# A hybrid SSD and neighbourhood-attention block: the scan in 16 steps with 2.5 pieces of the q, k, v projection each

## The chip, the cores and the metric

The kernel runs on one core of one Trainium2 chip. The metric is the device time in microseconds of one execution of the whole program, the median over several runs. The engines of the core are named as in the profile: PE (TensorE, matrix products into the PSUM banks), DVE (VectorE), ACT (ScalarE), POOL (GpSimd) and SP (SyncE, here the queue from which most DMA transfers are issued; ACT has a queue of its own). Each engine works through its own queue in order, and waits on semaphores for what others make.

## The reference, cut to what matters

One encoder layer over T = 1024 tokens of width 1024, all in float32:

```python
h = rmsnorm(x, norm_mix_w)
z, xbc, dt_raw, q, k, v = split(h @ w_in)           # 1024 | 1536 | 32 | 1024 | 1024 | 1024 columns
xs, B, C = split(silu(conv5(xbc)))                   # xs: 16 heads of 64; B, C: 2 groups of 128 states
dt_f, dt_b = softplus(dt_raw + dt_bias)              # one step size per token, head and direction
y = ssd(xs*dt_f, dt_f*a_f, B, C) + flip(ssd(flip(xs*dt_b), flip(dt_b*a_b), flip(B), flip(C))) + d_skip*xs
y_ssm = grouped_rmsnorm(y * silu(z)) * norm_w        # groups of 512 columns
y_na  = neighbourhood_attention(rmsnorm(q), rmsnorm(k), v, rel_pos_bias)
x = x + concat([y_ssm, y_na]) @ w_out
x = x + relu(rmsnorm(x) @ w1)**2 @ w2
```

`ssd` is a chunked scan. In each of 8 chunks of 128 tokens, with `a_cum` the running sum of the log decays:

```python
decay  = exp(where(lower, a_cum[l] - a_cum[s], -inf))        # per head, 128 x 128
y_diag = (C @ B.T * decay) @ xdt                             # inside the chunk
state  = B.T @ (xdt * exp(a_cum[-1] - a_cum))                # what the chunk adds
h      = exp(a_cum[-1]) * h + state                          # carried to the next chunk
y_off  = (C @ h_in) * exp(a_cum)                             # what comes from the chunks before
```

The backward direction is the same on the reversed sequence, so its states are carried from the last chunk to the first.

## The kernel before, in words

**Stages.** The program has these stages one after the other: transposing and splitting x; twelve x tiles (`xbc`, columns of the projection for xs, B and C, each followed by the convolution; B and C come first, then `decays`, then the eight tiles of xs); the gate z in two groups of 8 tiles of tokens; the scan together with the q, k, v projection; the attention with the output projection; the MLP in seven products per block. Exact float32 products are made of three matmuls on a high and a low part (`mm3`, lines 180 to 182; `split_from_psum`, lines 189 and 190): the high part is an ACT copy, the low part a DVE or POOL difference. Weights come as tiles of 128 x 1024 through SP's queue (line 149, `wraw`), are split by ACT (line 150, `wh`) and DVE (line 151, `wl`), and there are three raw buffers and four pairs of split ones, so that one group of 512 columns (four tiles) fills them.

**A piece** is one tile of 128 tokens of one group of 512 columns of q, k or v: 24 matmuls into a bank `mm` (three banks), and after it for q and k a norm (ACT, DVE, POOL), four transposes into a bank `tp` and a split, for v only a split, and stores from ACT's queue. Three projections with two groups of eight make 48 pieces, traced as one loop behind the scan.

**The scan before** goes over i = 0..7 and the groups g = 0, 1, and makes `backward(7 - i, g)` and then `forward(i, g)`:

- `backward` loads xs, makes C B (`pcb`, line 575, a bank `s`), and for each half of the group's 8 heads loads the running sums of both directions, broadcast to all partitions (`rb`, line 593), subtracts the token's own sum (two POOL operations, line 600), selects by the triangle (DVE, line 606), takes the exponential (ACT, line 611), multiplies by C B (DVE, line 613) and makes four heads' products (`pd`, line 618, the one bank `v`). One matrix per head so serves both directions, one in each triangle. Then it adds what the later chunks carry in (`carried`), sums it all up, and updates the backward state (`decay_state`): a weighing of xs on POOL, a split (lines 528 and 529), the products `pS`, POOL and DVE to update the state (lines 537 and 538), and a split of the state (lines 541 and 542).
- `forward` adds what the earlier chunks carry in, and updates the forward state in the same way.
- The half of y that is made first waits in `y1_dr` in DRAM until the other direction reaches that chunk. Then `gated` multiplies with silu(z), norms and stores.

`carried` splits C for each use (lines 550 and 551), multiplies with the split state (`py`, a bank `s`; there are two) and scales (`yo`, line 555, one buffer).

**What sets the order.** The tile framework puts every instruction into its engine's queue by a simulated timeline: an instruction is issued when its inputs are ready in that timeline, and of those ready, the one traced first. So before the change the q, k, v pieces fill PE wherever the planner expects the scan not to be ready. `tc.issue_after(ins)` adds an edge of order alone: what is traced in the block goes behind `ins` on its engine. Buffers are handed on tile by tile (`reuse_waits="tile"`): a new tile waits for the last use of what lay there. The attention's pools lie partly where the scan's tiles were.

Of the kernel before, what the change touches and what calls it, by code (L numbers as in the profile page):

```python
# [19 lines left out]
P = 128  # L20
T = 1024
D = 1024
# [34 lines left out]
def hymba_block(  # L57
# [66 lines left out]
    y1_dr = dr.tile([NT, P, D], F32, name="y1_dr")  # L124
# [54 lines left out]
    def mm3(pt, ah, al, bh, bl, first, last):  # L179
        nc.tensor.matmul(pt, lhsT=ah, rhs=bh, start=first, stop=False)  # L180
        nc.tensor.matmul(pt, lhsT=ah, rhs=bl, start=False, stop=False)  # L181
        return nc.tensor.matmul(pt, lhsT=al, rhs=bh, start=False, stop=last)  # L182

# [24 lines left out]
    with ExitStack() as ph:  # L208
# [21 lines left out]
        with ExitStack() as p0:  # L230
# [14 lines left out]
            for h in range(2):  # L245
# [31 lines left out]
                dg = rp.tile([P, 4, P], F32, tag="dg", name="dg")  # L277
# [29 lines left out]

        def proj_col(get, m, h, pt):
# [5 lines left out]
        with p1:  # L314
            qp = p1.enter_context(tc.tile_pool(name="qp", bufs=2, side="right", reuse_waits="tile"))
# [166 lines left out]
            for ft in range(8):  # L482
                xbc((ft,))


            szb = sz_dr.rearrange("c p f -> (c p) f").rearrange(
                "(i b j) f -> i b j f", b=8, j=8
            )
            for g in range(2):
                get = load_w_nat(w_in[0], 0, KD, OFF_Z + 512 * g, nc.vector)  # L490
                for t in range(NT):
                    pt = ps_mm("pz")
                    for k in range(KD):
                        s = (slice(None), k, slice(t * P, (t + 1) * P))
                        mm3(pt, hTh[s], hTl[s], *get(k), k == 0, k == KD - 1)
                    zs = qp.tile([P, 512], F32, tag="zs", name="zs")
                    nc.scalar.activation(zs, pt, AF.Silu, scale=rcol[:, t : t + 1])
                    nc.scalar.dma_start(szb[:, t, :, g * 512 : (g + 1) * 512], zs)

        def hb(v):  # L500
            return v.unsqueeze(2).broadcast_to([P, 8, HD])

        def h8(v):
            return v.rearrange("p (e d) -> p e d", d=HD)

        with ExitStack() as p2:
# [14 lines left out]
            st = [[None, None], [None, None]]  # L521

            def decay_state(d, c, g, xw):
                prev = st[d][g]
                pS = ps_s("pS")
                xh = qp.tile([P, 512], F32R, tag="xh", name="xh", bufs=1)
                xl = qp.tile([P, 512], F32R, tag="xl", name="xl", bufs=1)
                nc.scalar.activation(xh, xw, AF.Copy)
                nc.vector.tensor_tensor(xl, xw, xh.bitcast(F32), op=sub)
                mm3(pS, bNh[:, c, g, :], bNl[:, c, g, :], xh, xl, True, True)  # L530
                new = prev and prev[0]
                if prev is None:
                    new = qp.tile([P, 512], F32, tag=f"st{d}{g}", name="st", bufs=1)
                    nc.vector.tensor_copy(new, pS)
                else:
                    dec = ed[:, d, c, 8 * g : 8 * g + 8]
                    nc.gpsimd.tensor_tensor(h8(new), h8(new), hb(dec), op=mul)
# [183 lines left out]

# [680 lines left out]
```

## Time and profile before

| what | value |
|---|---|
| median of 3 runs | 1670.96 us (1668.05 to 1673.75) |
| the profiled execution: its time, its span | 1675.21 us, 1673.4 us |
| mean granted PE clock of the profiled execution | 0.988 |
| x tiles from `decays` on, about 84 to 172 us | 88 us, PE busy throughout |
| the gate z, 172 to 261 us | 89 us, PE busy throughout |
| scan with pieces, 261 to 600 us | 339 us, PE 306.0, DVE 270.0, POOL 264.5, ACT 134.9 us busy |
| pieces alone, 600 to 668 us | 68 us |

The table is read by stage: busy time of an engine in a stretch, against the stretch's length. A matmul of 512 columns is reported with about 390 ns, though in a dense stream one starts every 227 ns, because matmuls overlap; so for PE the distances between starts count, not the durations. Where a wait of PE is reported, it names the instruction that PE waited with and the one that released it.

### The profile page before, as it was taken

Reading aid. Unit: us, or ns where it says so; the run is one execution under the profiler, and the core shown is the slowest. Engines: PE = TensorE matmul, PEld = TensorE weight load, DVE = VectorE, ACT = ScalarE, POOL = GpSimd, SP = SyncE. Lnnn points to the kernel's source line nnn. Section 1 sums busy time; section 2 is a strip of 40 time slices with the busy share of each in tenths; the row PEclk is TensorE's granted clock in tenths of the full one; section 3 lists DMA queues with packets and bytes.
Section 4 is the critical chain, followed back from the end, with each engine's and each line's share of the span. In section 5 each row is a group of like instructions: output and inputs, shape, how many; then the busy total and the mean of one; then the engine's idle time right before and its main releaser. Section 6 shows DMA issues by size and latency. Waiting matters only on the chain. (4 is left out here: it accounts for less than half of the span.)

```text
span 1673.4 us, 20880 instructions
## 1 busy us (share of the span) xinstructions
PE 1594.3 (95%) x7462; PEld 1296.9 (78%) x7462; DVE 1027.3 (61%) x1432; ACT 722.5 (43%) x1195; POOL 721.8 (43%) x520
## 2 busy tenths in 40 slices
PE   7999999899998899999999989999999979999999
PEld 6788888777776677887887777788888868888887
DVE  4777214889796852666675567434243388887863
ACT  5434223434343442566665433554444444433330
POOL 3000004788688762233334232344444465455551
PEclk9999999999999999999999999999999999999999
DMA  8113337776666884987674240343354386644331
GB/s 206 52 38 114 87 99 226 208 193 195 223 216 185 225 266 176 279 212 204 174 208 133 89 164 38 138 164 131 133 166 149 129 295 230 219 145 151 101 101 76
DMA packets 181026, 273.49 MB, mean 163 GB/s; under 512 B 14691, under 2 KB 105915, under 8 KB 180923
## 3 DMA queue, kind: packets, MB, share of 16 engines
q1 hardware_dynamic: 136939, 231.26, 45.3%
q10 hardware_dynamic: 42976, 37.23, 7.3%
q0 software_dynamic: 1008, 3.67, 0.5%
q8 instruction: 59, 0.97, 0.2%
q14 instruction: 44, 0.36, 0.1%
HBM read 188.88 MB, written 86.56 MB: 165 GB/s over the span
## 5 line engine op out<-in xcount | busy, mean ns | idle before, releaser
L748 POOL TENSOR_TENSOR wl<-wraw,wh 128x1024 fp32r<-128x1024 f32 x110 | 298.8, 2728 | 318.4 <-ACT wh L747 305.1
L747 ACT ACTIVATE wh<-wraw 128x1024 fp32r<-128x1024 f32 x110 | 115.5, 1054 | 151.3 <-PE px L733 51.3
L733 PE MATMUL px<-wh,ahl 128*128 128x512 f32 x512 | 160.9, 391 | 4.6 <-ACT ahl L747 3.3
L180 PE MATMUL pq<-wh,hTh 128*128 128x512 f32 x384 | 152.7, 400 | 4.8 <-ACT wh L150 4.8
L181 PE MATMUL pq<-wl,hTh 128*128 128x512 f32 x384 | 152.3, 398 | 5.2 <-DVE wl L151 5.2
L733 PE MATMUL px<-h,wh 128*128 128x512 f32 x496 | 155.8, 394 | 1.4 <-DVE x L1089 1.4
L182 PE MATMUL pq<-wh,hTl 128*128 128x512 f32 x384 | 152.0, 397 | 0.0
L748 DVE TENSOR_TENSOR ahl<-ar,ahl 128x1024 fp32r<-128x1024 f32 x56 | 114.8, 2058 | 23.2 <-ACT ahl L747 22.1
L747 ACT ACTIVATE ahl<-ar 128x1024 fp32r<-128x1024 f32 x56 | 58.2, 1052 | 140.0 <-PE px L733 76.3
L733 PEld LDWEIGHTS px<-wh,ahl 128*128 128x128 f32 x512 | 96.1, 188 | 26.0 <-ACT ahl L747 3.7
L733 PEld LDWEIGHTS px<-h,wh 128*128 128x128 f32 x496 | 92.8, 187 | 24.4 <-ACT h L186 1.6
L151 DVE TENSOR_TENSOR wl<-wraw,wh 128x1024 fp32r<-128x1024 f32 x40 | 54.7, 1373 | 82.5 <-ACT wh L150 81.9
L733 PE MATMUL px<-wl,ahl 128*128 128x512 f32 x256 | 99.9, 390 | 0.0
L733 PE MATMUL px<-h,wl 128*128 128x512 f32 x248 | 97.8, 394 | 0.0
L181 PEld LDWEIGHTS pq<-wl,hTh 128*128 128x128 f32 x384 | 72.9, 190 | 22.2 <-DVE wl L151 8.0
L180 PEld LDWEIGHTS pq<-wh,hTh 128*128 128x128 f32 x384 | 72.8, 190 | 21.5 <-ACT wh L150 7.1
L186 ACT ACTIVATE pth<-ptp 128x384 fp32r<-128x384 f32 (+1 forms) x128 | 56.8, 456 | 67.1 <-PE ptp L947 66.6
L600 POOL TENSOR_TENSOR rb<-rb,c 128x512 f32<-128x512 f32 x64 | 76.1, 1210 | 20.3 <-DMA rb<-cum_dr 17.4
L182 PEld LDWEIGHTS pq<-wh,hTl 128*128 128x128 f32 x384 | 72.9, 190 | 14.7
L150 ACT ACTIVATE wh<-wraw 128x1024 fp32r<-128x1024 f32 x58 | 61.0, 1057 | 53.1 <-PE px L181 24.1
L733 PE MATMUL pz<-h,wh 128*128 128x512 f32 x256 | 81.9, 400 | 0.7 <-DVE h L187 0.7
L733 PE MATMUL pz<-wh,ahl 128*128 128x512 f32 x256 | 80.5, 391 | 0.0
(271 smaller groups left out, 4081.2 us busy)
## 6 DMA issues: line engine op xcount, KB each, us to landing
ar<-act_dr SPq DMA_DIRECT2D x56, 512.0 KB, 3.6
act_dr<-cq SPq DMA_DIRECT2D x49, 512.0 KB, 3.0
wraw<-in_w_in_dram SPq DMA_DIRECT2D x44, 512.0 KB, 4.3
rb<-cum_dr SPq DMA_DIRECT2D x32, 512.0 KB, 6.7
wraw<-in_w_mlp_in_dram SPq DMA_DIRECT2D x32, 512.0 KB, 4.6
wraw<-in_w_mlp_out_dram SPq DMA_DIRECT2D x32, 512.0 KB, 4.2
q_dr<-hl ACTq DMA_DIRECT2D x64, 128.0 KB, 3.0
k_dr<-hl ACTq DMA_DIRECT2D x16, 512.0 KB, 4.4
```

Source lines behind the costliest of these rows:

```text
L150: nc.scalar.activation(hi[:, 0:n], raw[:, 0:n], AF.Copy)
L151: lo_eng.tensor_tensor(lo[:, 0:n], raw[:, 0:n], hi[:, 0:n].bitcast(F32), op=sub)
L180: nc.tensor.matmul(pt, lhsT=ah, rhs=bh, start=first, stop=False)
L181: nc.tensor.matmul(pt, lhsT=ah, rhs=bl, start=False, stop=False)
L182: return nc.tensor.matmul(pt, lhsT=al, rhs=bh, start=False, stop=last)
L186: top = nc.scalar.activation(hi, src, AF.Copy)
L600: nc.gpsimd.tensor_tensor(rb[:, d], rb[:, d], c1[:, d, c, h0 : h0 + 4].unsqueeze(2).broadcast_to([P, 4, P]), op=sub,)
L733: nc.tensor.matmul(pt, lhsT=a, rhs=b, start=f, stop=l, skip_group_check=True)
L747: nc.scalar.activation(hl[0], src, AF.Copy)
L748: eng.tensor_tensor(hl[1], src, hl[0].bitcast(F32), op=sub)
```

## The change

The scan is laid out anew:

- **Exponents.** `segment` makes the differences of the decays for four heads of a chunk (broadcast load, two POOL subtractions, the DVE selection) and stores them to `seg_dr` in DRAM. One of the 32 is made after each of the eight x tiles of xs, one after each of the 16 tiles of z, and the last eight in the first eight steps of the scan. The exponential itself is taken after loading, in the scan.
- **Backward states.** Beside z, `state_in` loads xs, weighs and splits it, and two tiles of z later `state_out` makes the products, updates the running backward state and stores it to `sb_dr`, one for each of the 14 chunks that need one.
- **Steps.** The scan is now one pass over g and, inside it, c, 16 steps in forward order. `prepare` makes what a step needs besides the forward state (loads, exponentials, splits of C, of the stored backward state and of the weighed xs) and is traced a step ahead. `inside` makes C B (now in a bank `tp`), both `py` products and most of the sum; `carry` updates the forward state behind a piece; `finish` makes the heads' products behind the same piece, and the gating. `y1_dr` is gone; every chunk is finished in its step.
- **Pieces.** The q, k, v projection is a generator of 48 pieces. One is traced before the first step, two or three in each step, and the last seven after the scan.
- Buffers: `yo` has two, and the tiles for z move from the pool `qp` to `rp`.

```diff
+            def segment(pool, bufs, g, c, q):
+                h0 = 8 * g + 4 * q
+                rb = pool.tile([P, 2, 4, P], F32, tag="rb", name="rb", bufs=bufs)
+                r0 = c * 16 + h0
+                nc.sync.dma_start(
+                    rb.rearrange("p d h s -> p d (h s)"),
+                    cum_dr[:, r0 : r0 + 4, :]
+                    .rearrange("d h s -> d (h s)")
+                    .partition_broadcast(P),
+                )
+                for d in range(2):
+                    nc.gpsimd.tensor_tensor(
+                        rb[:, d],
+                        rb[:, d],
+                        c1[:, d, c, h0 : h0 + 4].unsqueeze(2).broadcast_to([P, 4, P]),
+                        op=sub,
+                    )
+                nc.vector.copy_predicated(
+                    rb[:, 0],
+                    lmask.unsqueeze(1).broadcast_to([P, 4, P]),
+                    rb[:, 1],
+                )
+                nc.sync.dma_start(seg_dr[g, c, :, q], rb[:, 0].rearrange("p h s -> p (h s)"))
+
+            segs = [(g, c, q) for g in range(2) for c in range(NT) for q in range(2)]
...
             for ft in range(8):
                 xbc((ft,))
+                segment(rp, 2, *segs.pop(0))
...
+            def weighed(pool, bufs, d, c, g, xs):
+                xw = pool.tile([P, 512], F32, tag="xw", name="xw", bufs=bufs)
+                hs = slice(8 * g, 8 * g + 8)
+                nc.gpsimd.tensor_tensor(h8(xw), h8(xs), hb(wd[:, d, c, hs]), op=mul)
+                hl = [pool.tile([P, 512], F32R, tag=f"x{i}", name="xhl", bufs=bufs) for i in "hl"]
+                split_to(hl, xw, nc.vector)
+                return hl
+
+            def state_in(c, g):
+                xs = zp.tile([P, 512], F32, tag="xs", name="xs")
+                nc.sync.dma_start(xs, xs_dr[c, :, g * 512 : (g + 1) * 512])
+                return c, g, weighed(zp, 2, 1, c, g, xs)
+
+            def state_out(c, g, hl):
+                pS = ps_s("pS")
+                mm3(pS, bNh[:, c, g, :], bNl[:, c, g, :], *hl, True, True)
+                new = zp.tile([P, 512], F32, tag="st", name="st")
+                if g not in sb:
+                    nc.vector.tensor_copy(new, pS)
+                else:
+                    nc.gpsimd.tensor_tensor(
+                        h8(new), h8(sb[g]), hb(ed[:, 1, c, 8 * g : 8 * g + 8]), op=mul
+                    )
+                    nc.vector.tensor_tensor(new, new, pS, op=add)
+                sb[g] = new
+                nc.sync.dma_start(sb_dr[g, c - 1], new)
...
                     nc.scalar.dma_start(szb[:, t, :, g * 512 : (g + 1) * 512], zs)
+                    n = 8 * g + t
+                    if n > 1:
+                        with tc.issue_after(mark.ins):
+                            state_out(*ready.pop(0))
+                    if n < 14:
+                        ready.append(state_in(NT - 1 - n % 7, n // 7))
+                    segment(rp, 2, *segs.pop(0))
...
+            def prepare(c, g):
...
+                nc.sync.dma_start(xs, xs_dr[c, :, gs])
+                for q in range(2):
+                    gm = qp.tile([P, 4, P], F32, tag=f"gm{q}", name="gm")
+                    nc.sync.dma_start(gm.rearrange("p h s -> p (h s)"), seg_dr[g, c, :, q])
+                    nc.scalar.activation(gm, gm, AF.Exp)
...
+                split_to(chl, ct, nc.vector)
+                if c < NT - 1:
...
+                    nc.sync.dma_start(raw, sb_dr[g, c])
...
+                    split_to(back, raw, nc.vector)
+                    xhl = weighed(qp, 1, 0, c, g, xs)
...
+            def inside(c, g, xs, gms, chl, sts):
+                pcb = ps_tp("pcb")
...
+                for d in sts:
+                    pys[d] = ps_s("py")
+                    mm3(pys[d], *chl, *sts[d], True, True)
...
+                nc.gpsimd.tensor_tensor(h8(y1), h8(xs), hb(cf), op=mul)
+                for gm in gms:
+                    nc.vector.tensor_tensor(
+                        gm, gm, cb.unsqueeze(1).broadcast_to([P, 4, P]), op=mul
+                    )
+                for d in sts:
+                    yo = qp.tile([P, 512], F32, tag="yo", name="yo")
+                    nc.vector.tensor_tensor(h8(yo), h8(pys[d]), hb(e1[:, d, c, hs]), op=mul)
+                    nc.gpsimd.tensor_tensor(y1, y1, yo, op=add)
+
+            def carry(c, g, xhl, mark):
+                pS = ps_s("pS")
+                with tc.issue_after(mark):
+                    mm3(pS, bNh[:, c, g, :], bNl[:, c, g, :], *xhl, True, True)
...
+                    nc.gpsimd.tensor_tensor(h8(st[g]), h8(st[g]), hb(dec), op=mul)
+                    nc.vector.tensor_tensor(st[g], st[g], pS, op=add)
+                hl = [qp.tile([P, 512], F32R, tag=f"s{i}", name="shl", bufs=1) for i in "hl"]
+                split_to(hl, st[g], nc.vector)
+
+            def finish(c, g, xs, gms, y1, mark):
+                pd = ps_v("pd")
+                with tc.issue_after(mark):
+                    for e in range(8):
+                        nc.tensor.matmul(
+                            pd[:, e * HD : (e + 1) * HD],
+                            lhsT=gms[e // 4][:, e % 4, :],
+                            rhs=xs[:, e * HD : (e + 1) * HD],
+                            start=True,
+                            stop=True,
+                        )
+                nc.vector.tensor_tensor(y1, y1, pd, op=add)
+                gated(y1, c, g)
...
+            steps = [(c, g) for g in range(2) for c in range(NT)]
+            held = prepare(*steps[0])
+            mark = next(units)
+            ahead = {}
+            for n, (c, g) in enumerate(steps):
+                xs, gms, chl, back, xhl = held
+                sts = {}
+                if back:
+                    sts[1] = back
+                if c > 0:
+                    sts[0] = ahead[g]
+                y1 = inside(c, g, xs, gms, chl, sts)
+                if n + 1 < len(steps):
+                    held = prepare(*steps[n + 1])
+                mark = next(units)
+                if xhl:
+                    ahead[g] = carry(c, g, xhl, mark)
+                finish(c, g, xs, gms, y1, mark)
+                mark = next(units)
+                if segs:
+                    segment(qp, 1, *segs.pop(0))
+                if n % 2:
+                    mark = next(units)
+            for mark in units:
+                pass
```

More of the change, by code (lines that the diff above doesn't have):

```diff
@@ L276, in hymba_block @@
                 nc.gpsimd.tensor_tensor(rcol[:, s], rcol[:, s], half[:, s], op=ALU.pow)
[L277 removed]
+                dg = rp.tile([P, 4, P], F32, tag="zs", name="dg", bufs=2)
                 nc.vector.tensor_tensor(
@@ L306, in hymba_block, with hb, h8 @@
         nc.sync.dma_start(dsk, d_skip.partition_broadcast(P)[:, 0, :])
+        def hb(v):
+            return v.unsqueeze(2).broadcast_to([P, 8, HD])
+        def h8(v):
+            return v.rearrange("p (e d) -> p e d", d=HD)
         def proj_col(get, m, h, pt):
@@ L494, in hymba_block @@
                         s = (slice(None), k, slice(t * P, (t + 1) * P))
-                        mm3(pt, hTh[s], hTl[s], *get(k), k == 0, k == KD - 1)
-                    zs = qp.tile([P, 512], F32, tag="zs", name="zs")
+                        mark = mm3(pt, hTh[s], hTl[s], *get(k), k == 0, k == KD - 1)
+                    zs = rp.tile([P, 512], F32, tag="zs", name="zs", bufs=2)
                     nc.scalar.activation(zs, pt, AF.Silu, scale=rcol[:, t : t + 1])
                     nc.scalar.dma_start(szb[:, t, :, g * 512 : (g + 1) * 512], zs)
[L500 to L504, printed above, removed]
+                    n = 8 * g + t
[5 more added lines that the diff above has]
+                    segment(rp, 2, *segs.pop(0))
         with ExitStack() as p2:
@@ L567, in gated @@
                 nc.scalar.dma_start(y_dr[c, :, gs], y1)
-            def backward(c, g):
+            def prepare(c, g):
+                gs = slice(g * 512, (g + 1) * 512)
+                xs = qp.tile([P, 512], F32, tag="xs", name="xs")
+                nc.sync.dma_start(xs, xs_dr[c, :, gs])
+                gms = []
+                for q in range(2):
+                    gm = qp.tile([P, 4, P], F32, tag=f"gm{q}", name="gm")
+                    nc.sync.dma_start(gm.rearrange("p h s -> p (h s)"), seg_dr[g, c, :, q])
+                    nc.scalar.activation(gm, gm, AF.Exp)
+                    gms.append(gm)
+                ct = cT[:, g, c * P : (c + 1) * P]
+                chl = [qp.tile([P, P], F32R, tag=f"c{i}", name="chl") for i in "hl"]
+                split_to(chl, ct, nc.vector)
+                back = None
+                if c < NT - 1:
+                    raw = qp.tile([P, 512], F32, tag="sb", name="sb", bufs=1)
+                    nc.sync.dma_start(raw, sb_dr[g, c])
+                    back = [
+                        qp.tile([P, 512], F32R, tag=f"b{i}", name="shl", bufs=1) for i in "hl"
+                    ]
+                    split_to(back, raw, nc.vector)
+                    xhl = weighed(qp, 1, 0, c, g, xs)
+                else:
+                    xhl = None
+                return xs, gms, chl, back, xhl
+            def inside(c, g, xs, gms, chl, sts):
                 hs = slice(8 * g, 8 * g + 8)
                 cs = slice(c * P, (c + 1) * P)
-                xs = qp.tile([P, 512], F32, tag="xs", name="xs")
-                nc.sync.dma_start(xs, xs_dr[c, :, g * 512 : (g + 1) * 512])
-                pcb = ps_s("pcb")
+                pcb = ps_tp("pcb")
                 nc.tensor.matmul(
```

186 lines of the change are left out of this document (53 added, 133 removed).

## The prediction

> **What bounds the kernel now.** I read the engine totals first, then busy time by stretches, then who waited for whom on TensorE (PE) in the stretch that the change rebuilds, and last the order of single matmuls, for the price of each kind. Totals and stretches:
>
> ```profile
> span 1673.4 us, 20880 instructions
> PE 1594.3 (95%) x7462; PEld 1296.9 (78%) x7462; DVE 1027.3 (61%) x1432; ACT 722.5 (43%) x1195; POOL 721.8 (43%) x520
> ...
> 84.00:172.00 88.00, 88.00 (x421) 73.16 (x420) 62.35 (x75) 37.44 (x43) 0.51 (x8) 1.00 0.27 78
> 172.00:261.00 89.00, 89.00 (x402) 73.90 (x401) 14.44 (x13) 23.24 (x29) 0.26 (x1) 1.00 0.32 88
> 261.00:600.00 339.00, 306.00 (x1452) 245.61 (x1451) 270.01 (x389) 134.88 (x240) 264.50 (x243) 0.97 0.73 212
> 600.00:640.00 40.00, 36.39 (x168) 29.17 (x167) 17.88 (x24) 13.80 (x21) 19.40 (x22) 1.00 1.01 306
> 640.00:668.00 28.00, 28.00 (x129) 23.27 (x129) 5.70 (x8) 6.72 (x9) 2.37 (x2) 1.00 0.36 139
> ```
>
> The columns of a stretch are its bounds and length, then busy us of PE, weight loads, DVE (VectorE), ACT (ScalarE) and POOL (GpSimd), the granted clock, the DMA share and GB/s. The x tiles (84 to 172) and the gate z (172 to 261) leave PE no idle time, and POOL has nothing to do there. From 261 to 600 the scan runs between the q, k, v pieces, and there PE idles for 33 us, DVE is busy for 80% and POOL for 78%. Then the rest of the pieces runs until 668. So PE is the bound, and only the 407 us from 261 to 668 hold time to win. Who held PE there:
>
> ```profile
> PE pd L618 <- DVE rb L613: 7.3, 7, 2.3
> PE pcb L575 <- DVE yo L555: 6.6, 4, 2.5
> PE pq L181 <- DVE wl L151: 5.2, 7, 1.8
> PE pq L180 <- ACT wh L150: 4.8, 4, 2.1
> PE pd L618 <- issue: 3.0, 1, 3.0
> PE py L180 <- DVE yo L555: 2.3, 2, 1.7
> PE ptq L693 <- DVE qn L687: 2.0, 5, 1.0
> PE py L181 <- DVE sl L542: 1.7, 2, 1.2
> PE py L180 <- DVE st L538: 1.0, 1, 1.0
> PE pS L180 <- ACT rb L611: 0.8, 1, 0.8
> PE ptq L693 <- ACT sz L564: 0.8, 1, 0.8
> PE pS L180 <- DVE st L538: 0.8, 1, 0.8
> ```
>
> After the colon stand the total us, the number of waits and the longest. The twelve rows add up to 36.3 us. Now the price of each kind of PE work, from the order in time:
>
> ```profile
> 280.41 1.10 PE L618 MATMUL pd<-xs,rb 128*128 128x64 f32 x8 [0.99 <-DVE rb L613]
> 281.32 0.48 PE L180 MATMUL pS<-xh,bNh 128*128 128x512 f32 x1
> ...
> 282.18 0.39 PE L575 MATMUL pcb<-cT,bT 128*128 128x128 f32 x2
> 282.40 0.60 PE L693 MATMUL ptq<-ident,qn 128*128 128x128 f32 x4
> 282.76 0.48 PE L180 MATMUL pq<-wh,hTh 128*128 128x512 f32 x1
> ...
> 308.71 0.39 PE L182 MATMUL pq<-wh,hTl 128*128 128x512 f32 x1
> ...
> 309.62 0.39 PE L180 MATMUL py<-sh,ch 128*128 128x512 f32 x1
> ...
> 310.30 0.39 PE L180 MATMUL pq<-wh,hTh 128*128 128x512 f32 x1
> ```
>
> The price is the distance between starts. Four matmuls go from 308.71 to 309.62, 0.227 us each, so a piece of 24 costs 5.45. Eight pd records (four heads) cost 0.91, a pS triple 0.86, pcb 0.22, four transposes 0.36, a py triple 0.68. By the loops there are 48 pieces (261.6), 16 steps with 8 heads (32 x 0.91 = 29.1), 28 pS and 28 py triples (24.1 and 19.0), 16 pcb (3.5) and 32 times four transposes (11.5): **349 us of bare PE work in 407 us**, so 58 us are lost. Of these, 36.3 are the named waits; the granted clock of 0.97 over 339 us is 10.2 more; the last 12 are refilling after a stop, switches between kinds, and a few early attention matmuls.
>
> **The change part by part.** Its arithmetic on PE is the same: 14 of the 28 state triples (pS) leave the scan for the gate, where PE is full, so 12 us only change place. I count them as nil.
>
> *Taken out of the scan.* What leaves, by the groups in 261 to 600:
>
> ```profile
> L606 DVE COPY_PREDICATED rb<-lmask,rb 128x512 f32<-128x512 int32 x32 | 40.6, 1268 | 15.9 <-POOL rb L600 15.8
> L529 DVE TENSOR_TENSOR xl<-xw,xh 128x512 fp32r<-128x512 f32 x28 | 25.3, 905 | 6.7 <-ACT xh L528 6.6
> L538 DVE TENSOR_TENSOR st<-st,pS 128x512 f32<-128x512 f32 x24 | 16.2, 675 | 0.0
> L600 POOL TENSOR_TENSOR rb<-rb,c 128x512 f32<-128x512 f32 x64 | 76.1, 1210 | 20.3 <-DMA rb<-cum_dr 17.4 <-PE ptq L693 2.4 <-PE pq L182 0.3
> L537 POOL TENSOR_TENSOR st<-st,ed 128x512 f32<-128x512 f32 x24 | 28.8, 1200 | 0.6 <-DVE sl L542 0.6
> L641 POOL TENSOR_TENSOR xw<-xs,wd 128x512 f32<-128x512 f32 x14 | 15.1, 1082 | 2.5 <-DMA xs<-xs_dr 2.5
> ```
>
> 24 of the 32 exponents go: 24 x 1.27 = 30 us of DVE and 48 x 1.21 = 58 of POOL. Half of the states go: 14 x 0.905 + 12 x 0.675 = 21 us of DVE, 12 x 1.2 + 15.1 = 30 of POOL. DVE falls from 270 to about 219, POOL from 264 to about 176. The backward state is still split once per step after its load, so that split stays counted.
>
> *Waits that go.* `pd` waits for the product with cb (7.3 us). The subtract, select and exponential that ran ahead of it in the same step now come a step early, and PE has a piece of 5.45 us between cb and pd; on DVE two products and two yo, four operations near 0.68, fit below it. Without that cover one product of 0.68 would show in each of 16 steps. `pcb` moves off the bank that yo had to free (6.6). The waits for st, sl and the exponential at py and pS (1.7 + 1.0 + 0.8 + 0.8 = 4.3) go because the state is a piece ahead. With a freer DVE I take 3 of the 10.0 us of weight splits at group changes; between none and all, the near end, as ACT and the load have part in them. The one unexplained 3.0 I leave, as I do the 2.3 of py for yo: both py of a step now fill the two `s` banks, so pS waits for a yo. That is 7.3 + 6.6 + 4.3 + 3 = 21. Given back: pcb now holds a `tp` bank until both products are done and the transposes have the other one alone; bounds 0 and the 6.6 it replaces, I take 2. **Gain 19.**
>
> *Clock.* 10.2 us are lost to the clock beside stops. With more than half of the stops gone I return 8; the bounds are 0 and 10.2.
>
> The Trainium skill ("TensorE: Matmul & The Clock Gate", the section on why it matters for kernels) says that the clock halves after an idle window of some 3.4 us, and advises no gaps over about 3 us. The trace differs: only one wait reaches 3.0, yet the clock dropped in several stretches. By the rule only that drop would be tied to a stop, and the sum would lose nearly all of the 8.
>
> *Fewer restarts* are worth 2 of the 12 left over (bounds 0 and 12).
>
> *Added beside the x tiles.* Eight exponents: each a broadcast load and a store on SP's queue, two POOL operations and a select. DVE gets 8 x 1.27 = 10 us on 62 of 88, and PE stays ahead of it.
>
> ```profile
> L606 DVE COPY_PREDICATED rb<-lmask,rb x32: 723/1558/1833, 274.9 to 592.1; 128x512 f32<-128x512 int32 x32
> L529 DVE TENSOR_TENSOR xl<-xw,xh x28: 670/689/1527, 272.8 to 557.4; 128x512 fp32r<-128x512 f32 x28
> ```
>
> Minimum, median and maximum show that DVE operations with two SBUF inputs take up to twice their own time or more where POOL works. I cost this at nothing; the cover is the 26 us that DVE idles.
>
> The Trainium skill ("SBUF — State Buffer", on the shared port pair) has DVE with two SBUF inputs and a reading POOL exclude each other for a whole instruction. The rows agree. If each of the 16 new POOL operations blocked the convolutions for its 1.21, DVE would need 62 + 10 + 19 = 92 of 88: 4 us more than nothing.
>
> *Added beside the gate.* DVE 14.4 + 16 x 1.27 + 21 = 56 of 89 us; POOL 38.7 for exponents and 30 for states, 69 of 89: both fit. PE takes the states two pieces late, 11 us of cover for a weighing (1.08), an ACT pass, a split (0.9) and the xs load. New stops there have no row; bounds 0 and 14 waits of 1.07 (36.3 us over 34 waits), 15 us. I take 3, nearer the bottom because of the two pieces.
>
> *After the scan.* Now 68 us remain from 600 to 668, and the attention's loads fill the DMA engines until 640. Afterwards 7 pieces remain, all of v, 7 x 5.45 = 38 us, where the loads took 40: the cover all but fits. Bounds 0 and 10, I take 2.
>
> Sum: 19 + 8 + 2 - 3 - 2 = **24 us**. The profiled execution took 1675.2 (span 1673.4 and 1.8 around it), so 1651; it lies 4.2 above the median of the runs, 1670.96, so I predict **1647**.
>
> **The rivals.** *A, all but bare.* DVE with 51 us less to do keeps every step below its PE work, and only group changes and switches remain. For it: 219 of DVE's and 176 of POOL's us against 337 of PE's. Against: the order is set beforehand by a planner's costs, and the doubled DVE times above are not constant. It would win 36.3 - 10.0 + 10.2 + 6 = 42 less 0 to 3: **1629**.
>
> *B, the waits form again.* pS and pd are bound behind a piece, so whatever DVE is late with stops the pieces behind it as well. A planner decides where each lands, and the exponents may not sit where the text puts them. 16 pd, 28 py and 14 pS leave 58 places; half of them at 1.07 us are 31 us, near the 36.3 that the waits cost now. For it: DVE's in-order queue still carries all splits. Gain 0 to 8: **1667**.
>
> *C, slower: SP's queue.* Weight loads share it, in order, with the new traffic: beside the gate's 8 weight tiles come 60 entries (a load and a store for each of 16 exponents and 14 states), and each store there waits for its DVE result. The trace shows the effect once, where the weights of the last group stood behind the attention's loads:
>
> ```profile
> 621.90 2.61 SPq L864 DMA_DIRECT2D braw<-t_dr  x1
> 624.61 0.41 SPq L149 DMA_DIRECT2D wraw<-in_w_in_dram  x1
> ...
> 633.98 0.98 PE L180 MATMUL pq<-wh,hTh 128*128 128x512 f32 x3 [2.15 <-ACT wh L150]
> ...
> wraw<-in_w_in_dram SPq DMA_DIRECT2D x44, 512.0 KB, 4.3
> ```
>
> If each of the 8 group changes (two of z, six of q, k, v) shows a load of 4.3 with its split, about 2.3 (6.6 together), that is 53 us against 10 now: 43 lost, 24 won, **1690**. It decides from 24 / 8 = 3 us extra per change. Against it: three raw buffers let loads run ahead, and the transfers fit (78 to 88 GB/s now, and by tile sizes 24 x 0.75 + 14 x 0.5 = 25 MB more in 177 us, 306 reached elsewhere).
>
> **How the numbers follow.** My forecast, 1647 with its own range of 1635 to 1660, has 0.50; A 0.18; B 0.17; C 0.15. 0.3%, 5 us, is about what a measurement tells from no change: faster is below 1666, slower above 1676. B splits into 0.06, 0.08 and 0.03; C gives 0.01 to same; the rest follows its sign. Faster 0.74, same 0.09, slower 0.17. For eight times in ten I take **1622 to 1680**: below lies the part of A that also keeps the weight waits (0.06), above most of C (0.12).
>
> **What would show it.** Right: in the scan's stretch the granted clock is 0.99 or more, PE's waits for the cb product and for yo are gone, the sum of its waits is below 20, DVE is near 219 us; z takes about 100 us and the x tiles still 88. Wrong: PE waits for weights at group changes over 3 us each (C); the waits at pd, py, pS stay near 30 us (B); or PE stands idle in the x or z stretch, or after the last piece.

## The result, and the profile after

The changed kernel takes **1686.47 us** (median, 1681.69 to 1688.69) against 1672.38 of the kernel before in the same series (1668.05 to 1676.83): the ratio is 1.0081, 95% interval 1.0059 to 1.0104. It is slower by 14 us, where 24 us of gain were forecast, and the time lies above the whole range. The profiled execution took 1681.69 (span 1679.9), the lowest of its runs, so its trace shows 6.5 us of the 14.

The page after, with the totals and the groups of the exponents' subtractions (L340) and selections (L346); idle time before a group and its releaser stand at the end of a row:

```profile
PE 1596.7 (95%) x7462; PEld 1303.9 (78%) x7462; DVE 1013.2 (60%) x1420; ACT 720.3 (43%) x1183; POOL 711.7 (42%) x520
...
L340 POOL TENSOR_TENSOR rb<-rb,c 128x512 f32<-128x512 f32 x64 | 70.5, 1123 | 121.0 <-DMA rb<-cum_dr 108.4
...
L346 DVE COPY_PREDICATED rb<-lmask,rb 128x512 f32<-128x512 int32 x32 | 35.6, 1113 | 84.5 <-POOL rb L340 77.1
```

DVE now stands idle for 84.5 us ahead of selections, 15.9 before, and POOL for 121.0 ahead of subtractions, 20.3 before. The next view is busy time by stretches (columns as in the prediction), with the bounds set at PE's first matmul of the gate z (181.8), its first of the pieces (313.3) and the end of the last piece:

```profile
84.00:181.80 97.80, 92.50 (x426) 75.76 (x424) 63.46 (x78) 34.86 (x41) 18.65 (x24) 0.97 0.41 117
181.80:313.30 131.50, 108.84 (x445) 86.67 (x443) 63.91 (x62) 34.81 (x48) 66.06 (x60) 0.91 0.74 224
313.30:676.10 362.80, 349.31 (x1706) 289.94 (x1705) 226.30 (x356) 144.87 (x244) 193.25 (x192) 0.98 0.70 216
```

Measured by the starts of PE's matmuls (the gate from its first matmul to its last, and all up to the last one of the pieces as the third stage), the stages went as follows (us; the gate before has 12 us added for the 14 backward states that moved there, and the pieces 12 taken off; the last of the 14 in fact follows the gate's last matmul, 0.9 us):

| stage | before, at equal work | after | difference |
|---|---|---|---|
| x tiles, from 84 | 88.2 | 97.8 | +9.6 |
| gate z | 88.6 + 12 = 100.6 | 130.6 | +30.0 |
| scan and pieces, to the last piece | 407.3 - 12 = 395.3 | 363.8 | -31.5 |
| all behind the last piece | 1005.3 | 1003.8 | -1.5 |

The scan gave back more than was forecast (31.5 against 29), and the two stages in which PE had never stopped lost 40. Who held PE there (total us, number of waits, longest), first for 84 to 313 us:

```profile
PE pS L181 <- ACT xhl L186: 8.1, 1, 8.1
PE pz L182 <- DVE wl L152: 7.6, 4, 5.4
PE ptx L503 <- ACT acc L495: 5.0, 4, 2.8
PE pS L181 <- DVE st L553: 3.4, 1, 3.4
PE ptx L503 <- ACT xn L510: 3.0, 1, 3.0
PE pS L182 <- DVE xhl L187: 0.8, 1, 0.8
...
PE ptq L717 <- DVE qn L711: 4.9, 4, 1.9
PE pd L686 <- issue: 2.2, 1, 2.2
PE pq L182 <- DVE wl L152: 1.1, 2, 0.8
PE pq L181 <- ACT wh L151: 1.1, 1, 1.1
```

The lines behind the dots are from 313 to 680 us. The first six add up to 27.9 us, where none stood before. The clock adds to it. Its mean of 0.91 over the gate's 131.5 us would be 11.8 us lost, but part of that fell into times in which PE stood anyway: counted in slices of half a microsecond, and only for the time that PE worked, it is 7.8 us in the gate and 3.0 in the x tiles. Together with the waits that is 38.7 of the 39.6 that the two stages lost.

What lies behind two of these waits shows in the order in time (start, duration, engine, instruction, and in brackets the idle time before it and what ended it):

```profile
181.12 0.36 SPq L333 DMA_DIRECT2D rb<-cum_dr  x1
...
182.37 1.04 ACT L151 ACTIVATE wh<-wraw 128x1024 fp32r<-128x1024 f32 x1
...
183.88 1.27 DVE L491 SCALAR_TENSOR_TENSOR acc<-ub,pcol,acc 128x1024 f32<-128x1024 f32 x1
...
187.54 2.04 POOL L340 TENSOR_TENSOR rb<-rb,c 128x512 f32<-128x512 f32 x2 [4.95 <-DMA rb<-cum_dr]
...
189.62 0.73 DVE L346 COPY_PREDICATED rb<-lmask,rb 128x512 f32<-128x512 int32 x1 [4.47 <-POOL rb L340]
190.24 1.27 DVE L491 SCALAR_TENSOR_TENSOR acc<-ub,pcol,acc 128x1024 f32<-128x1024 f32 x1
190.37 0.33 SPq L351 DMA_DIRECT2D seg_dr<-rb  x1
...
193.22 1.22 DVE L152 TENSOR_TENSOR wl<-wraw,wh 128x1024 fp32r<-128x1024 f32 x1
...
194.49 0.80 PE L182 MATMUL pz<-wl,hTh 128*128 128x512 f32 x1 [5.39 <-DVE wl L152]
...
195.58 0.36 SPq L333 DMA_DIRECT2D rb<-cum_dr  x1
...
210.74 0.59 ACT L510 COPY xn<-ptx 128x512 f32<-128x512 f32 x1 [0.27 <-PE ptx L503]
...
214.37 1.99 SPq L351 DMA_DIRECT2D seg_dr<-rb  x2
216.44 2.36 SPq L333 DMA_DIRECT2D rb<-cum_dr  x2
218.85 0.46 SPq L515 DMA_DIRECT2D xs_dr<-xn  x1
...
224.62 1.54 DVE L346 COPY_PREDICATED rb<-lmask,rb 128x512 f32<-128x512 int32 x1 [8.63 <-POOL rb L340]
...
226.20 0.33 SPq L351 DMA_DIRECT2D seg_dr<-rb  x1
226.62 0.88 SPq L540 DMA_DIRECT2D xs<-xs_dr  x2
...
231.60 0.63 ACT L186 ACTIVATE xhl<-xw 128x512 fp32r<-128x512 f32 x1 [13.48 <-POOL xw L533]
...
232.29 0.80 PE L181 MATMUL pS<-xhl,bNh 128*128 128x512 f32 x1 [8.09 <-ACT xhl L186]
```

The first stop: ACT had made the high part of a weight tile at 183.41. The low part (L152) stands in DVE's queue behind a selection that comes to the head at 185.15 and waits 4.47 us for POOL, and then behind taps of the convolution that were held up with it (L491). It starts at 193.22, and PE has stood for 5.39 us. The second: the last tile of xs is stored at 218.85, 39 us behind the last product of its projection (179.7); before it was 188.6 against 171.9. ACT had it ready at 211.33, and for the last 7.5 us its store stood in SP's queue behind two exponents' stores and two of their loads. The load of xs for the first backward state then stands there behind the store of one more exponent, which waits for a selection that waited 8.63, and is issued 7.3 us after the last tile's store. (It needs only the first four of the eight tiles; in e4 below it follows that store within 0.5 us, at 194.43 behind 193.97.) So PE, which must make that state's product ahead of the next tile of z, stands for 8.09.

The first lines also show one buffer's round trip. It is loaded from 181.12, subtracted from 187.54, selected from 189.62, stored from 190.37, and loaded again at 195.58, with the other buffer's load between the two (at 189.39): 14.5 us for one round, 7.2 for each exponent with two buffers.

### The profile page after: what moved, and what is told of

Its sections match the earlier page's. It is cut to its first block, busy times and chain, and to the rows that moved or that the text cites. A ratio compares the mean times of both kernels' runs of the same rounds, so it can differ in the third digit from the quotient of the medians.

```text
span 1679.9 us, 20923 instructions
## 1 busy us (share of the span) xinstructions
PE 1596.7 (95%) x7462; PEld 1303.9 (78%) x7462; DVE 1013.2 (60%) x1420; ACT 720.3 (43%) x1183; POOL 711.7 (42%) x520
## 5 line engine op out<-in xcount | busy, mean ns | idle before, releaser
L340 POOL TENSOR_TENSOR rb<-rb,c 128x512 f32<-128x512 f32 x64 | 70.5, 1123 | 121.0 <-DMA rb<-cum_dr 108.4
L914 POOL TENSOR_TENSOR mb<-braw,nam 128x256 f32<-128x256 f32 (+1 forms) x48 | 38.5, 830 | 116.3 <-DMA braw<-t_dr 74.1
L181 PEld LDWEIGHTS pq<-wh,hTh 128*128 128x128 f32 x384 | 73.2, 191 | 17.4 <-ACT wh L151 1.4
L346 DVE COPY_PREDICATED rb<-lmask,rb 128x512 f32<-128x512 int32 x32 | 35.6, 1113 | 84.5 <-POOL rb L340 77.1
```

What stands on the lines that cost most here:

```text
L340: nc.gpsimd.tensor_tensor(rb[:, d], rb[:, d], c1[:, d, c, h0 : h0 + 4].unsqueeze(2).broadcast_to([P, 4, P]), op=sub,)
L346: nc.vector.copy_predicated(rb[:, 0], lmask.unsqueeze(1).broadcast_to([P, 4, P]), rb[:, 1],)
L914: nc.gpsimd.tensor_tensor(mb[:, s].rearrange("p (s r c) -> p s r c", r=16, c=8), v[:, a:b], nam[:, s].rearrange("p (s r c) -> p s r c", r= ...
```

## The experiments

The theories, by the letters that the expectations use. **H**: a selection that comes too early to the head of DVE's in-order queue holds up what stands behind it, taps, weight splits and state sums. **R**: the ring of two `rb` buffers with its round trip, and SP's order, set the pace of the exponents, and PE's stops follow from it. **L**: POOL's new work slows DVE's operations. **S**: the state's products, bound two tiles behind, stop PE by themselves. All intervals are 95%; each ratio is to the kernel before on the same chip.

### e1: the selections a tile later

`segment` is cut in two: `differences` (load, subtractions) and `select` (selection, store).

```diff
                 xbc((ft,))                                  # x tiles
-                segment(rp, 2, *segs.pop(0))
+                with tc.issue_after(tap.ins):               # tap: the last of the next tile's convolution
+                    select(made)
+                made = differences(rp, 2, *segs.pop(0))
...
-                    segment(rp, 2, *segs.pop(0))            # gate
+                    with tc.issue_after(tap.ins):           # tap: the sum of the next state
+                        select(made)
+                    made = differences(rp, 2, *segs.pop(0))
```

> Same work as the changed kernel; only the DVE selects of the 24 exponents beside the x tiles and the gate are issued later: beside x behind the last convolution tap of the next tile, beside z behind the sum of the next backward state. Theory H (a select stands at the head of DVE's in-order queue until its broadcast load and its two POOL differences are done, and the taps and weight splits behind it are late): PE's 24 us of waits between 84 and 313 us fall below 10, DVE's 84 us of idle time ahead of the selects falls below half, the gate ends about 25 us earlier, 1655 to 1665 us. Rival L (POOL working beside the taps slows DVE itself): 1686, as nothing is done less. Rival R (two rb buffers and SP's queue set the pace of the exponents): 1680 to 1690, the selects only move the wait.

Measured: 1675.03 us, ratio 1.0016 (1.0001 to 1.0031), 11 us under the changed kernel, between the ranges of H and R. Busy time by stretches, x tiles and gate:

```profile
84.00:173.60 89.60, 88.91 (x422) 73.19 (x421) 68.16 (x78) 35.99 (x41) 16.20 (x19) 1.00 0.41 115
173.60:297.60 124.00, 108.72 (x443) 86.38 (x443) 59.26 (x56) 33.46 (x46) 64.80 (x57) 0.93 0.74 222
```

The x tiles are back at 89.6 with all eight exponents still beside them, and the clock there is full. So it was the place in DVE's queue that cost 8.2 of the 9.6, as H says. In the gate the same edit helped less: 119.8 between its first and last matmul, 19 too many, and PE's waits of the two stages fell from 27.9 to 15.8 us, not below 10.

### e2: four buffers of their own beside the gate

```diff
-                    segment(rp, 2, *segs.pop(0))
+                    segment(zp, 4, *segs.pop(0))
```

> The 16 exponents beside the gate get four rb buffers instead of sharing two with those beside the x tiles. Rival R (the ring of two buffers sets the pace): the gate's stretch shortens by 15 us or more, 1665 to 1672 us. Theory H: loads start earlier, so selects wait less, but those among the taps of the x tiles stay: 5 to 10 us, 1676 to 1682. Rival L: 1686.

Measured: 1660.26 us, ratio 0.9932 (0.9907 to 0.9958): faster than before, and better than even R's range. The gate fell from 130.6 to 107.6, the x tiles stayed slow (99.9).

### e6: a ring of its own, but of two

```diff
-                    segment(zp, 4, *segs.pop(0))            # against e2
+                    segment(zp, 2, *segs.pop(0))
```

> As the run with four buffers beside the gate, but two in that pool. Tells apart what the four buffers did. If the number of buffers was it (rival R): the gate goes back to 120 to 130 us, 1672 to 1685. If it was the place (in the pool that opens after the x tiles they cannot be taken ahead and fill the ring and DVE's queue while convolutions still run): gate 106 to 112, 1658 to 1664.

Measured: 1679.8 us, ratio 1.0044 (1.0024 to 1.0063). Between e2 and e6 only the number of buffers differs: 19.5 us. The selections in the gate, their number, and the first and last start; first in the changed kernel, then in e6, then in e2:

```profile
L346 DVE COPY_PREDICATED rb<-lmask,rb x13: 728/1575/1595, 212.8 to 298.2; 128x512 f32<-128x512 int32 x13
```

```profile
L346 DVE COPY_PREDICATED rb<-lmask,rb x16: 730/1561/1640, 212.5 to 320.9; 128x512 f32<-128x512 int32 x16
```

```profile
L346 DVE COPY_PREDICATED rb<-lmask,rb x16: 741/1572/1596, 213.6 to 286.0; 128x512 f32<-128x512 int32 x16
```

One exponent every 85.4 / 12 = 7.1 us, 108.4 / 15 = 7.2 us, and with four buffers 72.4 / 15 = 4.8 us. Two buffers give the 7.2 of the round trip above, more than a tile of z with its state's products (5.45 + 0.86 = 6.3), and the text of the program has one exponent to a tile. So the exponents fall behind, and what stands behind a selection on DVE, or behind its store on SP, falls behind with them. In e6 they ran past the gate into the first pieces, where one weight split came 11.8 us late for PE. So the loss was not where R had put it: e6's gate took 113.7 and not 120 to 130, and the stage of the pieces 380.6 against 363.6 in e2.

SP's own waits show one way in which a short ring does harm. A load into a buffer waits until the store of what it held has landed, and all that stands behind it in SP's queue waits too. Total us, number and longest of these waits from 172 to 310 us, in e6 and then in e2:

```profile
SPq L333 <- DMA seg_dr<-rb: 39.6, 13, 5.7
```

```profile
SPq L333 <- DMA seg_dr<-rb: 8.1, 3, 5.7
```

### e5: both cures

Selections a tile later beside the x tiles only, four buffers beside the gate.

> The changed kernel with two orders: beside the x tiles each select is issued behind the next tile's last tap, and the 16 exponents beside the gate have four rb buffers of their own in the pool that opens after the x tiles. If the two cures act in different places (x tiles 99.9 us in the four-buffer run, 89.6 in the run with later selects; gate 107.6 there), they add: x tiles 90, gate 105 to 108, the rest 364, 1646 to 1652 us. If they are one effect seen twice: no better than 1660.

Measured: **1654.01 us**, ratio 0.9891 (0.9869 to 0.9912): x tiles 89.1, gate 111.1, scan and pieces 362.8. The two cures all but add up: e2 alone had taken 26.2 us off the changed kernel and e1, which also moved the selections beside the gate, 11.4; together they took 32.5, and the time lies 2 us above the range for that case.

### e3 and e7: none beside the x tiles

Sixteen exponents beside the gate, sixteen in the scan; e3 with the old ring, e7 with four buffers in the gate's own pool.

```diff
                 xbc((ft,))
-                segment(rp, 2, *segs.pop(0))
...
                 if n % 2:
                     mark = next(units)
+                    if segs:
+                        segment(qp, 1, *segs.pop(0))
```

> No exponents beside the x tiles; 16 beside the gate, 16 in the scan's steps. Theory H and rival L: the x tiles end near 172 us again and the stop at the first state goes, as xs is stored in time; the gate still carries selects, but no taps behind them: 1660 to 1668 us. Rival S (the state products, issued two tiles after their loads, are what stops PE beside the gate): the waits at pS stay near 12 us, 1675 to 1680. The scan's steps carry 8 more exponents at up to 3 us each of new waits: 0 to 10 us against it.

Measured: 1690.26 us, ratio 1.0104 (1.007 to 1.0138), and the x tiles took 97.7 all the same. The selections of the gate, by their first and last start:

```profile
L346 DVE COPY_PREDICATED rb<-lmask,rb x16: 727/748/1589, 137.4 to 235.0; 128x512 f32<-128x512 int32 x16
```

The gate begins at 182. The planner had pulled the exponents that the text puts beside the gate up between the x tiles, since their inputs were ready and their buffers free. So e3 did not test what it was made for. e7 did, because its buffers exist only once the x tiles have released theirs:

> No exponents beside the x tiles, this time also none pulled there by the planner, since the 16 beside the gate lie in the pool that opens after the x tiles (four buffers); 16 in the scan. Theory H: x tiles 88 us as before the change, gate 105 to 108, the scan with 8 exponents more 370 to 382: 1654 to 1666 us. If the x tiles were slow for another reason than the exponents, they stay near 98: 1665 to 1675.

Measured: 1665.22 us, ratio 0.9959 (0.9944 to 0.9974). The x tiles by busy time:

```profile
84.00:172.90 88.90, 88.90 (x425) 73.86 (x425) 63.26 (x76) 37.88 (x45) 0.51 (x8) 1.00 0.26 78
```

PE has no gap there. The gate took 106.5; the scan, with eight exponents more, 381.4.

### e4: the exponents back in the scan

```diff
-                segment(rp, 2, *segs.pop(0))                # x tiles
...
+                    if n > 11:                              # gate: the last four tiles only
                         segment(rp, 2, *segs.pop(0))
...
-                if segs:
-                    segment(qp, 1, *segs.pop(0))
+                for _ in range(2):
+                    if segs:
+                        segment(qp, 2, *segs.pop(0))
```

> The exponents' move is undone but for four beside the last gate tiles that the first two steps need: 28 are made in the scan, two in a step. States stay beside the gate. Theory H: x tiles and gate take about 88 and 100 us as forecast, PE's waits there fall below 5 us; the scan's DVE rises by 25 us to about 255, still below PE: 1650 to 1660 us. Rival S: waits at pS stay near 12 us and the total is 1670. If the exponents' place had made the scan faster, the stretch behind the gate, 363 us now, would grow by 20 us or more: 1670 to 1680.

Measured: 1674.6 us, ratio 1.0011 (0.9992 to 1.0031), no difference from the kernel before, as the last of the three expectations has it. Gate, and scan with pieces:

```profile
177.00:276.30 99.30, 99.30 (x443) 81.67 (x442) 35.12 (x41) 33.54 (x46) 31.21 (x27) 1.00 0.49 157
276.30:670.00 393.70, 358.60 (x1700) 293.19 (x1699) 255.45 (x374) 141.88 (x242) 239.26 (x231) 0.96 0.80 239
```

This run says two things. The gate with all 14 states leaves PE no idle time: 98.4 between its first and last matmul, against the 100.6 worked out (99.8 with the 13 products that lie in it), so the states alone cost no more than their products there (S is not needed to explain the loss). POOL's 27 operations are 14 weighings and 12 products of the states, and one clearing of a tile; the planner had pulled the four exponents up between the x tiles, which took 93.0. And the scan in its new layout, with the exponents in it, takes 395.0, the 395.3 of before at equal work. The 16 steps alone are worth nothing here; the gain came with the exponents' leaving. One thing is not equal, though: e4's exponents still go through `seg_dr` in DRAM and back, those of the kernel before did not.

### e8: the old scan, with the exponents moved

The kernel before, with 24 selections made beside the x tiles (a tile later) and the gate (four buffers); the scan's layout and its states stay as they were.

```diff
                     h0 = 8 * g + 4 * q                      # in backward
-                    rb = qp.tile([P, 2, 4, P], F32, tag="rb", name="rb", bufs=2)
...
+                    if (g, c, q) in early_segs:
+                        gm = qp.tile([P, 4, P], F32, tag="gm", name="gm", bufs=2)
+                        nc.sync.dma_start(gm.rearrange("p h s -> p (h s)"), seg_dr[g, c, :, q])
```

> The kernel before with one part of the change alone: 24 exponents made beside the x tiles and the gate (in the cured order, four buffers beside the gate), loaded in the old scan; its layout, its states, its bank of pcb and the place of the pieces as before. If what the scan won (407 us less 12 of moved states to 364) came from DVE and POOL being freed of exponents: the stretch from the gate to the last piece falls from 407 to 370 to 380, and the total is 1645 to 1655. If it came from the layout (inputs a step ahead, pieces bound to steps, pcb in another bank): the stretch stays at 395 or more and the total is 1665 to 1680.

Measured: 1665.55 us, ratio 0.9953 (0.9936 to 0.9971): 6.6 us of gain from the exponents alone. The stretch behind the gate:

```profile
278.30:660.80 382.50, 365.73 (x1746) 298.89 (x1745) 251.52 (x395) 155.55 (x270) 222.80 (x218) 0.97 0.69 213
```

By the starts of matmuls it fell from 407.3 to 382.8, near the first expectation, while the total lies in the second: what the exponents cost beside the x tiles and the gate, 4.1 and 13.1 us even in the cured order, took most of it back. The new layout with the states takes another 11.5 off (e5); in its scan that is 8.0 us at equal work (382.8 - 12 = 370.8 against 362.8). So the layout is worth something once most of the exponents are gone, and nothing before.

### e10 and e12: the stores from POOL's queue

```diff
-                nc.sync.dma_start(
+                nc.gpsimd.dma_start(
                     seg_dr[g, c, :, q], rb[:, 0].rearrange("p h s -> p (h s)")
                 )
```

> The changed kernel (1686.5), two buffers, only the store of each exponent issued from POOL's queue instead of SP's. If SP's order holds the loads back (a store that waits for its select stands ahead of the next load): exponents beside z every 5 us instead of 7.0, gate 120 or less against 130.6, time 1675 or less. If the two buffers and their round trip set the pace, the order of SP is nil: 7 us each, 1680 to 1690. A third way: POOL now waits for the select before its next subtraction, the chain gets longer, and the time is 1690 or more.

Measured (the changed kernel with this edit): 1685.9 us, ratio 1.0086 (1.0066 to 1.0106), nothing won. The 15 selections from 201.8 to 313.2 come one every 111.4 / 14 = 8.0 us. Taking the stores out of SP's queue does not quicken the exponents. The test is not clean. POOL now waits for the selection ahead of its own next subtraction, as the third expectation has it; and SP's queue was not freed, since the loads into the two buffers, which stayed there, still wait for those stores to land (68.1 us between 180 and 309). What the run excludes is that the move pays.

> The fifth run's kernel (1654.0) with the same move of the exponents' stores to POOL's queue. With four buffers the round trip has slack: if the loads were still held back behind stores, gate 106 or less against 111.1 and 1648 to 1651; if not, 1654 within 2; if POOL's waits for selects reach the scan or the states, 1657 or more.

Measured (e5 with this edit): 1659.44 us, ratio 0.9929 (0.9909 to 0.995), somewhat slower than e5, with intervals that just overlap; the third expectation.

### e9: the states a tile later

e5, with `if n > 1` made `if n > 2` ahead of `state_out`, three buffers for the split xs, and the last state behind the gate.

> The fifth run's kernel (selects beside x a tile later, the z exponents in four buffers of their own) with the state's products beside z traced three tiles of z behind its loading instead of two. Its first run took 1654.0, and PE's only named waits beside z (8.6 us) were mostly at pS for the split of the weighed xs. If the late states stop PE there (S, held false so far): those waits fall below 3 and the time is 1646 to 1650. If the waits only change place: 1654 within 2.

Measured: **1647.84 us**, ratio 0.9861 (0.9838 to 0.9884), the lowest median of all, 23.6 us under the kernel before (by the interval 19 to 27). Its interval overlaps that of e5. PE's waits from the x tiles to the end of the gate, in e5 and then in e9:

```profile
PE pS L181 <- ACT xhl L186: 4.2, 4, 1.7
PE pz L182 <- DVE wl L152: 2.1, 4, 0.8
PE pz L181 <- ACT wh L151: 1.2, 1, 1.2
PE pS L182 <- DVE xhl L187: 0.9, 3, 0.4
```

```profile
PE pz L182 <- DVE wl L152: 4.5, 4, 1.9
...
PE pS L182 <- DVE xhl L187: 0.4, 1, 0.4
...
PE pS L181 <- ACT xhl L186: 0.2, 1, 0.2
```

The waits at pS fell from 5.1 to 0.6, and part of them came back at the weights. The sum, 8.4 in e5 and 6.5 here, did not fall below 3, as was expected for S. The time came out as S said, but only in part for its reason: of the 9.0 us between the two traces 4.3 lie in the gate (111.1 and 106.8; 0.9 of them one product that moved behind it), the x tiles took 2.0 more, and 5.8 lie behind the last piece (1005.6 and 999.8), where nothing was changed and where the other kernels take between 1000.6 and 1005.6. So S may hold for some 3 us in the gate once H and R are cured; that it makes the kernel faster is not shown, and the third buffer for the split xs, which came with it, was not tried alone. Stages of e9:

```profile
84.00:175.10 91.10, 90.57 (x429) 74.53 (x428) 69.76 (x81) 37.06 (x42) 16.87 (x22) 1.00 0.40 113
175.10:283.50 108.40, 102.21 (x443) 80.90 (x442) 70.24 (x61) 33.03 (x46) 80.87 (x62) 1.00 0.88 280
```

## Why the prediction was wrong

**The step that failed** is the cost of the exponents beside the x tiles and the gate. It took 0 and 3 us, because DVE's and POOL's busy times fitted into their stretches ("both fit", for the gate); measured were 9.6 and 30.0, the second past the bound of 15 that was given. PE standing idle in these two stretches was the last of the signs of being wrong that the prediction named itself. Busy times did fit, and still do: in the gate DVE was busy for 63.9 of 131.5 us and POOL for 66.1, close to the 56 and 69 that were forecast, but for 89 us. Added up were five short operations. Not added up was that they form one chain over three queues (SP, POOL, DVE and SP again), with two buffers, at 14.5 us a round, and that SP's and DVE's queues also carry, in order, what PE waits for. The hint stood in rows that the prediction quotes for their durations: in the scan before, 15.9 us of idle DVE ahead of the selections, and 20.3 us of idle POOL, 17.4 of them for the broadcast load. There the operations were counted as leaving the scan; the waits went along with them.

**"The cover is the 26 us that DVE idles"** took idle time for room. DVE works its queue in order, and can use such time only for an operation whose input is there: in the lines above it stood 4.47 us at a selection with taps and a weight split behind it. In the x tiles DVE's idle time grew from 26 to 34 us (63.5 busy of 97.8), while the convolutions ran late. e1 left the work there and moved it one tile back in the queue, and most of the cost was gone.

**The scan's terms** held in sum, 29 forecast and 31.5 measured, not one by one:
- Waits: 36.3 became 13.5 in the new scan, 22.8 won against 19. (They were 36 waits of 1.01 us on average, not 34 of 1.07; the bound of 15 would be 14, which changes nothing.) `pcb` behind yo is gone, and `pd` waits 0.6 us for its product; weights take 2.2 instead of 10.0 (3 were hoped for). Given back were 2.9 at the transposes (`ptq` behind qn, 4.9 against 2.0), 2 forecast.
- Clock: 8 forecast, about 3 won (0.98 over 362.8 us is 7 still lost of 10.2). The stops got fewer, but the clock still fell beside some of those left.
- The rest, "fewer restarts", 2 forecast, is 31.5 - 22.8 - 3, between 5 and 6.
- "DVE falls to about 219": 226.3 in 363 us.

e4 corrects the reading of this sum: with the exponents left in, the new layout wins none of it. The waits of `pd` for the product with cb and of `pcb` for yo are gone there too, as the prediction said of the layout. But others have formed in their place, above all 10.6 us at weight splits and 7.8 at pS behind yo, and their sum from 276 us on is 34.7, next to the 36.3 of before. In e8, with the old layout and fewer exponents, the same two waits all but go (0.2 and 0.5). So each part of the change takes them away; only with DVE and POOL relieved does nothing as large come back.

**After the scan**, 2 forecast: no loss is seen (1005.3 became 1003.8 behind the last piece, within what this stretch varies by).

**The rivals.** C's 1690 lies next to the measured time, but not for its reason. It had weights late at group changes, 53 us; they wait 7.6 + 2.2 = 9.8 us against 10 before, and the one long wait among them (5.39) was for DVE. Its sentence that stores wait for their DVE result in SP's queue was right for another load, that of xs at 226.62. B's remark that a planner may not leave the exponents where the text puts them is what happened in e3, and its waits that form again are what e4 shows. A did not come: 13.5 us of waits stay in the scan. One more rival, that the added traffic fills the DMA engines, is ruled out by the lines above: they were busy for 0.74 of the gate at 224 GB/s in the changed kernel, and for 0.88 at 280 GB/s in e9's shorter one.

**L**, the shared port (Trainium skill, "SBUF — State Buffer", section "SBUF: two separate sides"), had been priced at 4 us more by the rule. Mean time of a tap of the convolution between 84 and 190 us, before, after and in e9 (line, group, busy, mean ns):

```profile
L451 DVE SCALAR_TENSOR_TENSOR acc<-ub,pcol,acc 128x1024 f32<-128x1024 f32 x32 | 40.8, 1282 | 5.8 <-ACT acc L443 5.0
```

```profile
L491 DVE SCALAR_TENSOR_TENSOR acc<-ub,pcol,acc 128x1024 f32<-128x1024 f32 x25 | 32.3, 1310 | 3.9 <-ACT acc L483 3.9
```

```profile
L497 DVE SCALAR_TENSOR_TENSOR acc<-ub,pcol,acc 128x1024 f32<-128x1024 f32 x33 | 48.5, 1470 | 2.8 <-ACT acc L489 2.4
```

In the slow kernel they are hardly longer, in e9 they are longer by 0.19 us each, 6 us for 33, and its x tiles lose 2.9 at most. With no exponents beside them (e7) the mean is 1282 again; and in e9's order in time each tap or run of taps of well over 1.28 us apiece lies beside a subtraction of POOL (one of 2.04 us at 140.11 beside those from 136.54 to 141.08). So POOL does lengthen them, as the rule says, and this is not where the time went.

**What stays open**: how the 19.5 us between two and four buffers divide between the broadcast load, SP's order and DVE's queue. SP's waits are seen (39.6 us with two buffers, 8.1 with four), but not how much of them reached PE. Moving the stores to POOL, and with them POOL's own waits, could not part them; stores and loads on a queue that nothing else uses were not tried.

## What to carry to other kernels

Work that is moved beside a stage which keeps PE full is to be priced by the round trip of its buffers, not by busy time alone: one round (load, every operation, store, and the waits between) divided by the number of buffers should be shorter than the time that the stage gives each item. Here it was 14.5 / 2 = 7.2 against 6.3, and with four buffers an item came every 4.8. And ask of each of its operations what stands behind it in the same in-order queue; put it there so late that its input has come (one tile later won 11 us here), and give it buffers that the planner can't use earlier than meant.

## What the runs showed of the hardware that was not expected

The granted clock raised the price of the gate's stops by a third. In slices of half a microsecond it read 1.00 or 0.50 in the changed kernel, with a mixture only where it turned. After each of the five stops of 2.8 to 8.1 us in the x tiles and the gate it was 0.50 for some time: the stop of 5.39 us ended at 194.49, and the clock was full again only from 198.1 on. In the gate this cost 7.8 us of PE's work, beside 22.6 us in which PE stood. In e9, whose waits there are at most 1.9 us, the clock is 1.00. The Trainium skill ("TensorE: Matmul & The Clock Gate", section "Why this matters for your kernels") advises against gaps of PE of more than about 3 us, since one such window of idling brings the clock back to half; that agrees with these two stages. But in the changed kernel's scan a stop of 2.2 us was enough: it ended at 354.78, and the clock was 0.50 from 355.1 to 358.5.
